# Two-layer hybrid decoder trunk on one core: standing halves of the last down projection 128 bytes apart, three transfers held back, the convolution's middle sums in tiles of their own, query and key weights at four places

## The chip, the cores and the metric

The kernel runs on one core of one Trainium2 chip. The metric is the device time of one execution in microseconds (us). Three runs of the kernel before took 1107.52, 1106.53 and 1103.94 us; the median is 1106.53. One execution was profiled, and all rows below come from it. TensorE (PE) multiplies; VectorE (DVE) and ScalarE (ACT) work on tiles in SBUF and PSUM; GpSimd (POOL) and SyncE (SP) mostly issue DMA transfers, each on a queue of its own.

## The reference, cut to what matters

512 tokens of width 1024 go through two layers in float32. Layer 0 mixes tokens with 16 attention heads, layer 1 with a gated short convolution. Both end in the same kind of MLP, with `w_up` of 1024 x 5632 and `w_down` of 2816 x 1024.

```python
proj = rms_norm(h, norm_g) @ w_in            # layer 0: queries, keys, values, 8 gates
h = h + attention(proj) @ w_out              # layer 0
y = gate_b * causal_dwconv(gate_c * u, conv_w)   # layer 1: gate_b, gate_c, u = thirds of xn @ w_in
h = h + y @ w_out                            # layer 1
u = causal_dwconv(rms_norm(h, ffn_norm) @ w_up, ffn_conv)   # both layers
h = h + (silu(u[..., :2816]) * u[..., 2816:]) @ w_down      # both layers
```

## The kernel before

**Products.** Every float32 operand of a large product is split into a high and a low half that PE can take: ACT copies the high half (`whi`, L327 or L1045), DVE subtracts it from the operand and leaves the low half (`wlo`, L328 or L1047). PE then makes three products for each pair of blocks: high with high, high with low, low with high. Of the two operands of a matmul one stands in the array (128 x 128), the other moves through it (128 x 256 or 128 x 512). In a row of the profile such as `psb<-act,whi` the operand that moves is named first, the one that stands last.

**Sevens.** The up projections, the convolution's input projection and the down projections work on 2 x 2 blocks with seven products in place of eight. In the class `Sevens` (both up projections and, under the name "c", the convolution) a group g of 128 output columns is seven slots named p1, p7, p3, p6, p2, q5, q4, of 24 matmuls of 128 x 256 each. The weights of each slot are sums of the four blocks of w: the tiles X, Y, Z and W of a group are loaded from DRAM, and the sums are made partly by DVE, partly by transfers that POOL issues and that add to what the tile holds. In the convolution (five groups, 0 to 4) the middle sum Y + X is made by DVE in the tile Y itself (L1162), between the split of p7 and POOL's transfer that adds to X; the slot q5 needs that X. W and Z go through the three buffers of the pool `raw`.

**Standing and moving.** In `Sevens` and in layer 0's down projection the weights stand and the activations move. In layer 1's down projection, the last stage, it is the other way: the activations (`act`, split by `operand`) stand, the weights move. The tile `act` holds its high and low halves 2048 bytes apart in both layers. The weight tiles `whi` and `wlo` are tiles of `CHUNK` = 1056 floats, 4224 bytes, and where `load` puts one of the two `ASIDE` = 32 floats in, the offset between halves moves by 128 bytes.

**Down projection.** Seven phases (one per product) of six steps (`GROUPS`, one or two blocks of 128 rows each, 11 blocks together), 132 matmuls of 128 x 256 a phase, 924 in all. In layer 0 the weights of the phase q4 for the steps 3 to 5 are brought by POOL as added transfers, while SP loads those of the phase p3.

**Order.** Each engine works in program order. A scheduler decides the order ahead of time from the instructions' place in the code, with `pin` and `behind` fixing some of it; `behind(a, b)` puts a after b.

**Stages of the profiled execution** (us from the span's start): attention to 255, its output projection and the norm to 275, layer 0's first up groups (plain) to 316, layer 0 up in `Sevens` to 490, layer 0 down to 603, convolution to 735, its output projection to 770, layer 1 up to 985, layer 1 down to 1103.

Of the kernel before, what the change touches and what calls it, by code (L numbers as in the profile page):

```python
# [57 lines left out]
def trunk(  # L58
# [208 lines left out]
    wanted, ready, at, halve, aside = [], [], [0], {}, set()  # L267
# [9 lines left out]

    def bring(i):
        place, nk, n, blocks, queue = wanted[i]
        raw = place()  # L280
        if raw is None:
            raw = wp.tile([P, CHUNK], F32, tag="raw", name=f"raw{i}")
        v = raw[:, 0:nk * n].rearrange("p (k c) -> p k c", c=n)
        for (dram, k0, c0), fresh in blocks:
# [5 lines left out]
            elif not fresh or queue:  # L290
                tc.keep_in_program_order(
                    nc.gpsimd.dma_start(v, src, **({} if fresh else {"accum_op": ALU.add})))
            else:
                nc.sync.dma_start(v, src)
# [8 lines left out]
    def load(i):  # L303

        hi, lo = weight_tiles(i)
        begins = (0, 0)
# [160 lines left out]
    def want_qk(p):  # L467
        want(w_in, 0, 8, D + p * P, P)
        want(w_in, 0, 8, p * P, P)
# [631 lines left out]
    class Sevens:  # L1101

        def __init__(self, name, mp, groups, block_of):
            self.name, self.mp, self.groups, self.block_of = name, mp, groups, block_of
            self.forms = {n: [mp.tile([P, 4, HT], F32R, tag=f"{n}_{i}", name=f"{n}_{i}{name}") for i in ("hi", "lo")] for n in FORMS}
            self.st, self.wides, self.table, self.scaled = {}, {}, None, False

# [50 lines left out]

        def first_sums(self, g):
            self.weights_of(g, "p7", "Y")  # L1160
            if not self.table:
                self.summed = dve.tensor_tensor(self.st[g]["Y"], self.st[g]["Y"], self.st[g]["X"], op=ALU.add)  # L1162
# [13 lines left out]
        def slot(self, g, s):  # L1176
# [21 lines left out]
            elif s == 1:  # L1198
                first = not was
                if on and first and not self.ahead and "p6" not in c:  # L1200
                    self.weights_of(g, "p6", "three" if self.table else "Y")
# [4 lines left out]
                if on and not first and not self.table:  # L1206
                    self.weights_of(g, "p6", "Y")
                if soon and not self.table:
                    self.add_block(g + 1, "Y", 1, 1)
            elif s == 2:  # L1210
                if on:
# [3 lines left out]
                    c["four"] = c["three" if self.table else "Y"]  # L1215
# [4 lines left out]
            elif s == 3:  # L1220
                if was:
                    self.early(p, st[p]["R"])
                if on:
                    self.weights_of(g, "q5", "X")
                    if not self.table:
                        self.kept(g, "Xs", c["R"])
                        self.weights_of(g, "q4", "four")
            elif s == 4:
# [5 lines left out]
            if s == 5:  # L1234
                if on:
                    self.load_one(g, "Z", self.block_of(g, 1, 1))
                    self.open_wides(g)
                    if soon and not self.table:
                        self.weights_of(g + 1, "p1", "X")
                    self.left(g, c["A"])  # L1240
# [10 lines left out]
        chores, credit, ahead = (), 0.0, False  # L1251
# [141 lines left out]
    def conv_seven(norm, mp, rp):  # L1393
# [6 lines left out]
        up.norm, up.chores, up.ahead = norm, [], True  # L1400
# [50 lines left out]
        def tail(p, s):  # L1451
            u, c = (wides[p][n] for n in ("yg", "yv"))
            if p == 4:
# [6 lines left out]
                elif s == 3:  # L1460
                    halves_in(6, 2)
# [7 lines left out]
            elif s in (3, 4):  # L1469
                if s == 3:  # L1470
                    dve.tensor_tensor(u, u, both(row2), op=ALU.mult)
                if p < 3 or s == 3:
                    conv(2 * p + s - 3, u[:, s - 3, :])
# [71 lines left out]
    def mlp(layer, norm, mp, begun_up=None):  # L1545
# [36 lines left out]
        if layer == 0:  # L1582
            want_conv()
# [5 lines left out]
        def operand(i):  # L1589
# [5 lines left out]
            t = acts[i] = mp.tile([P, 2, 2, HT], F32R, tag=act_tags[i % 4], name=f"act{layer}_{i}")  # L1595
# [238 lines left out]
```

## Time and profile before

| | |
|---|---|
| runs | 1107.52, 1106.53, 1103.94 us; median 1106.53 |
| profiled execution | 1107.02 us, of which the span is 1105.2 |
| PE busy | 1088.8 us, 99% of the span |
| DVE busy | 959.6 us, 87% |
| ACT busy | 685.3 us, 62% |
| POOL busy | 181.1 us, 16% |

The span is the time from the first to the last instruction that the profiler saw; 1.8 us lie outside it. PE has work nearly all the time, so a share of 99% does not tell whether it works at its best pace. Matmuls overlap: a row gives some 280 ns for one of 128 x 256, but they start about 113 ns apart. So the number of matmuls in a stretch tells more of PE than its busy time does.

### The profile page before, as it was taken

Reading aid. Unit: us, or ns where it says so; the run is one execution under the profiler, and the core shown is the slowest. Engines: PE = TensorE matmul, PEld = TensorE weight load, DVE = VectorE, ACT = ScalarE, POOL = GpSimd, SP = SyncE. Lnnn points to the kernel's source line nnn. Section 1 sums busy time; section 2 is a strip of 40 time slices with the busy share of each in tenths; the row PEclk is TensorE's granted clock in tenths of the full one; section 3 lists DMA queues with packets and bytes.
Section 4 is the critical chain, followed back from the end, with each engine's and each line's share of the span. In section 5 each row is a group of like instructions: output and inputs, shape, how many; then the busy total and the mean of one; then the engine's idle time right before and its main releaser. Section 6 shows DMA issues by size and latency. Waiting matters only on the chain.

```text
span 1105.2 us, 21688 instructions
## 1 busy us (share of the span) xinstructions
PE 1088.8 (99%) x8781; PEld 1034.4 (94%) x8781; DVE 959.6 (87%) x1482; ACT 685.3 (62%) x1020; POOL 181.1 (16%) x206
## 2 busy tenths in 40 slices
PE   9999999999999999999999999999999999999998
PEld 7888787879999999999999899999999999999998
DVE  5798898997898888899979889877899899999886
ACT  7466667655466776776547655445666656567653
POOL 4011111111012211014401001001121121114300
PEclk9999999999999999999999999999999999999999
DMA  7678867789667988899964865698879887799951
GB/s 198 168 186 194 206 169 186 197 213 238 190 149 196 215 193 217 210 259 225 236 177 110 202 166 127 132 277 190 209 195 215 184 209 184 214 276 206 233 143 58
DMA packets 178116, 214.21 MB, mean 194 GB/s; under 512 B 7676, under 2 KB 143916, under 8 KB 178016
## 3 DMA queue, kind: packets, MB, share of 16 engines
q0 software_dynamic: 53280, 95.34, 44.9%
q1 hardware_dynamic: 124576, 117.42, 33.4%
q8 instruction: 69, 1.13, 0.4%
q14 instruction: 31, 0.25, 0.1%
q10 hardware_dynamic: 160, 0.07, 0.0%
HBM read 205.72 MB, written 44.04 MB: 226 GB/s over the span
## 4 chain that ended last, share of the span: by engine, by line
PE 64%; DVE 15%; issue 12%; DMA 6%; ACT 2%; POOL 0%; DVEq 0%; POOLq 0%; ACTq 0%
PE psb L351 14%; PE psb L1096 12%; PE psb L1710 10%; PE psa L1710 8%; PE psa L1096 5%; PE psa L351 3%; DMA three<-in_ffn_w_up 3%; DVE wlo_p L1047 3%; PE psb L727 2%; DMA Xc<-in_conv_w_in 2%; PE psa L824 2%; DVE wlo L328 2%; PE psc L799 1%; DVE ug L460 1%; PE psb L609 1%
## 5 line engine op out<-in xcount | busy, mean ns | idle before, releaser
L1096 PE MATMUL psb<-p_hi,wlo_p 128*128 128x256 f32 x480 | 132.5, 276 | 0.9 <-DVE wlo_p L74 0.9
L1096 PE MATMUL psb<-p_lo,whi_p 128*128 128x256 f32 x480 | 132.6, 276 | 0.0
L1096 PE MATMUL psb<-p_hi,whi_p 128*128 128x256 f32 x480 | 132.6, 276 | 0.0
L327 ACT ACTIVATE whi<-raw 128x1024 fp32r<-128x1024 f32 (+2 forms) x77 | 78.9, 1026 | 67.1 <-PE psb L351 22.5
L328 DVE TENSOR_TENSOR wlo<-raw,whi 128x1024 fp32r<-128x1024 f32 (+2 forms) x77 | 90.9, 1180 | 23.4 <-ACT whi L327 20.1
L351 PE MATMUL psb<-hs_a,whi 128*128 128x512 f32 (+1 forms) x312 | 93.3, 369 | 0.0
L1096 PE MATMUL psa<-p_hi,wlo_p 128*128 128x256 f32 x320 | 90.0, 281 | 1.8 <-DVE wlo_p L1047 1.7
L1096 PEld LDWEIGHTS psb<-p_hi,wlo_p 128*128 128x128 f32 x480 | 90.0, 188 | 1.2 <-DVE wlo_p L74 1.2
L1096 PE MATMUL psb<-q_hi,wlo_q 128*128 128x256 f32 x320 | 89.3, 279 | 1.3 <-DVE wlo_q L1047 1.3
L1096 PEld LDWEIGHTS psb<-p_hi,whi_p 128*128 128x128 f32 x480 | 90.1, 188 | 0.0
L1096 PEld LDWEIGHTS psb<-p_lo,whi_p 128*128 128x128 f32 x480 | 90.1, 188 | 0.0
L1096 PE MATMUL psa<-p_hi,whi_p 128*128 128x256 f32 x320 | 89.2, 279 | 0.2 <-ACT whi_p L1045 0.2
L1096 PE MATMUL psb<-q_hi,whi_q 128*128 128x256 f32 x320 | 88.9, 278 | 0.2 <-ACT Xs L1157 0.2
L1096 PE MATMUL psa<-p_lo,whi_p 128*128 128x256 f32 x320 | 89.0, 278 | 0.0
L1096 PE MATMUL psb<-q_lo,whi_q 128*128 128x256 f32 x320 | 88.6, 277 | 0.0
L351 PE MATMUL psb<-hs_a,wlo 128*128 128x512 f32 (+1 forms) x208 | 69.5, 359 | 0.0
L1096 PEld LDWEIGHTS psa<-p_hi,wlo_p 128*128 128x128 f32 x320 | 60.6, 189 | 2.9 <-DVE wlo_p L1047 2.4
L351 PEld LDWEIGHTS psb<-hs_a,whi 128*128 128x128 f32 x312 | 52.4, 188 | 10.3 <-issue 3.2
L1096 PEld LDWEIGHTS psb<-q_hi,wlo_q 128*128 128x128 f32 x320 | 60.2, 188 | 1.9 <-DVE wlo_q L1047 1.7
L1710 PE MATMUL psb<-act,whi 128*128 128x256 f32 x352 | 60.9, 277 | 0.9 <-DVE act L1049 0.7
L1096 PEld LDWEIGHTS psa<-p_hi,whi_p 128*128 128x128 f32 x320 | 60.6, 190 | 0.4 <-ACT whi_p L1045 0.4
L1096 PEld LDWEIGHTS psb<-q_hi,whi_q 128*128 128x128 f32 x320 | 60.3, 189 | 0.6 <-ACT Xs L1157 0.4
(544 smaller groups left out, 3699.8 us busy)
## 6 DMA issues: line engine op xcount, KB each, us to landing
t<-in_ffn_w_up POOLq DMA_DIRECT2D x24, 768.0 KB, 7.8
raw<-in_attn_w_in SPq DMA_DIRECT2D x24, 512.0 KB, 4.8
t<-in_ffn_w_up POOLq DMA_DIRECT2D x12, 1024.0 KB, 10.2
X<-in_ffn_w_up SPq DMA_DIRECT2D x20, 512.0 KB, 5.0
Y<-t SPq DMA_DIRECT2D x20, 512.0 KB, 6.6
three<-t SPq DMA_DIRECT2D x20, 512.0 KB, 5.6
W<-in_ffn_w_up SPq DMA_DIRECT2D x20, 512.0 KB, 4.0
Z<-in_ffn_w_up SPq DMA_DIRECT2D x20, 512.0 KB, 5.5
```

Source lines behind the costliest of these rows:

```text
L327: return (act.activation(hi_, raw[:, at_], AF.Copy), dve.tensor_tensor(lo_, raw[:, at_], f32(hi_), op=ALU.subtract))
L328: dve.tensor_tensor(lo_, raw[:, at_], f32(hi_), op=ALU.subtract))
L351: made = [pe.matmul(acc[:, c], w[x], rhs[y][:, c], start=first and x + y + c.start == 0, stop=last and x == 1 and c.stop == S) for x, y in ...
L460: made.append(dve.scalar_tensor_tensor(dst[:, d:], src[:, 0:S - d], tap(j), dst[:, d:], op0=ALU.mult, op1=ALU.add))
L609: pe.matmul(acc, lhs[0], w[0], start=first, stop=False)
L727: pe.matmul(ss[e][:, c:c + wide], ql[rows, b * P:n], kl[rows, 0:wide], start=first and b == bs[0], stop=last and b == bs[-1])
L799: pe.transpose(t[:, k * P:(k + 1) * P], w[:, e, k * P:(k + 1) * P], ident)
L824: pe.matmul(out_, w, t[:, first:first + step * (NB - k - 1) + 1:step, :], start=k == 0 and i == 0, stop=k == NB - 1 and i == 1)
L1047: rest = dve.tensor_tensor(lo, src, f32(hi), op=ALU.subtract)
L1096: pe.matmul(to, w[a][:, k, c], x[b][:, k, :], start=fresh and i + k + t == 0, stop=i == 1 and k == 3 and t == 2, skip_group_check=not fresh)
L1710: pe.matmul(part, l, r[:, c], start=begin and o + t + c.start == 0, stop=end and t == 2 and o + c.start > 0, skip_group_check=not fresh)
```

## The change

1. In layer 1's down projection the two halves of the standing tile `act` are put 128 bytes further apart (2048 + 128), the high half first in every second step and the low half first in the others. In layer 1's up projection the forms p6 and p2 of the activations get the 128 bytes too (`form_tile`).
2. In layer 0's down projection POOL runs a tiny addition (`hold`) that reads the tile into which SP loads step 3 of the phase p3, ahead of the three transfers of q4. They are thus issued only when that load has landed.
3. In the convolution's groups 1, 2 and 3 the sum Y + X goes into a tile `three` from the pool `raw`, behind the split of p1 (`three_of`), so that POOL's added transfer to X no longer comes after a sum in Y, and `raw` holds three tiles a group where it held two. SP's loads change their order: X1, Y1, Z0, X2, Y2, W1, Y3 where it was X1, Y1, Z0, W1, Z1, X2, Y2. The convolution's tail waits behind the split of q4.
4. The last piece of the convolution's output is split by two instructions of 128 x 512 on each of ACT and DVE in place of one of 128 x 1024 (`halves_in(6, 1)`, `halves_in(7, 1)`).
5. The weight tiles of queries and keys start 0, 32, 64 or 96 bytes into their buffers, high and low half alike.
6. In the first `Sevens` group of layer 0 the weights of p2 are split in slot 1, not in slot 2.
7. In the first group of layer 1 the next group's p7 weights are split ahead of the join of yv (`begins`).

```diff
-                tc.keep_in_program_order(
-                    nc.gpsimd.dma_start(v, src, **({} if fresh else {"accum_op": ALU.add})))
+                added = nc.gpsimd.dma_start(v, src, **({} if fresh else {"accum_op": ALU.add}))
+                tc.keep_in_program_order(added)
+                if i in landed:
+                    hold, other = tiny.tile([P, 1], F32, tag="hold", name=f"hold{i}", bufs=1), raws[landed[i]][:, 0:1]
+                    held_ = pool.tensor_tensor(hold, other, other, op=ALU.add)
+                    behind(added, held_)
...
-        begins = (0, 0)
+        begins = (shifted.get(i, 0),) * 2
...
-        want(w_in, 0, 8, p * P, P)
+        for i in (1, 0):
+            shifted[len(wanted)] = 8 * ((p + 2 * i) % 4)
+            want(w_in, 0, 8, i * D + p * P, P)
...
-            self.forms = {n: [mp.tile([P, 4, HT], F32R, tag=f"{n}_{i}", name=f"{n}_{i}{name}") for i in ("hi", "lo")] for n in FORMS}
+            self.forms = {n: [self.form_tile(mp, n, i) for i in ("hi", "lo")] for n in FORMS}
             self.st, self.wides, self.table, self.scaled = {}, {}, None, False
+
+        def form_tile(self, mp, n, i):
+            if self.name == 1 and n in ("p6", "p2"):
+                t, c = mp.tile([P, CHUNK], F32R, tag=f"{n}_{i}", name=f"{n}_{i}{self.name}"), ASIDE if i == "lo" else 0
+                return t[:, c:c + 1024].rearrange("p (k c) -> p k c", c=HT)
+            return mp.tile([P, 4, HT], F32R, tag=f"{n}_{i}", name=f"{n}_{i}{self.name}")
...
+        def sum_of(self, g):
+            return "three" if self.table or g in self.aside else "Y"
+
+        def three_of(self, g):
+            c = self.st[g]
+            c["three"] = wp.tile([P, CHUNK], F32, tag="raw", name=f"three{self.name}{g}")[:, 0:1024].rearrange("p (k c) -> p k c", c=2 * P)
+            behind(dve.tensor_tensor(c["three"], c["Y"], c["X"], op=ALU.add), self.rest)
+
         def first_sums(self, g):
+            c = self.st[g]
             self.weights_of(g, "p7", "Y")
-            if not self.table:
-                self.summed = dve.tensor_tensor(self.st[g]["Y"], self.st[g]["Y"], self.st[g]["X"], op=ALU.add)
+            if not self.table and g not in self.aside:
+                self.summed = dve.tensor_tensor(c["Y"], c["Y"], c["X"], op=ALU.add)
             self.add_block(g, "X", 0, 1)
             if self.table:
                 self.load_one(g, "three", self.table("6", g))
...
+                if on and first and self.name == 0:
+                    self.weights_of(g, "p2", "W")
...
+                        if g + 1 in self.aside:
+                            self.three_of(g + 1)
...
+                begins = self.name == 1 and not was
+                if soon and begins:
+                    self.first_sums(g + 1)
                 if on:
                     self.join(g, "yv", c["R"], c["P7s"])
-                if soon:
+                if soon and not begins:
...
-        up.norm, up.chores, up.ahead = norm, [], True
+        up.norm, up.chores, up.ahead, up.aside = norm, [], True, (1, 2, 3)
...
-                    halves_in(6, 2)
+                    halves_in(6, 1)
+                    halves_in(7, 1)
...
+            landed[begun + 6 * len(GROUPS) + 3] = begun + 4 * len(GROUPS) + 3
...
-            t = acts[i] = mp.tile([P, 2, 2, HT], F32R, tag=act_tags[i % 4], name=f"act{layer}_{i}")
-            halves_to(t[:, 0, 0:nk, :], t[:, 1, 0:nk, :], blocks.block(name, k0, nk), sign, held=("act", "dve") if p else ())
+            t = mp.tile([P, CHUNK if layer else 1024], F32R, tag=act_tags[i % 4], name=f"act{layer}_{i}")
+            hi, lo = acts[i] = [
+                t[:, c:c + 2 * HT].rearrange("p (k c) -> p k c", c=HT)
+                for c in (((0, 2 * HT + ASIDE), (2 * HT + ASIDE, 0))[i % 2] if layer else (0, 2 * HT))]
+            halves_to(hi[:, 0:nk, :], lo[:, 0:nk, :], blocks.block(name, k0, nk), sign, held=("act", "dve") if p else ())
```

In DVE's program at layer 0's first `Sevens` group `hs_a_wide` are the causal convolution's partial results of plain columns, `W` the loaded weight block, `wlo_p` the low half that the slot p2 needs and `wlo_q` that of the slots q5 and q4. Before:

```order
L1362 TENSOR_TENSOR hs_a_wide_4104<-psc_3897,nrow_n_3618 128x512
L1362 TENSOR_TENSOR hs_a_wide_4104<-psc_3956,nrow_n_3618 128x512
L460 SCALAR_TENSOR_TENSOR hs_a_wide_4104<-hs_a_wide_4104,taps 128x511 x2
L460 SCALAR_TENSOR_TENSOR hs_a_wide_4104<-hs_a_wide_4104,taps 128x510 x2
L460 SCALAR_TENSOR_TENSOR hs_a_wide_4104<-hs_a_wide_4104,taps 128x511
L1047 TENSOR_TENSOR wlo_p_4096<-W_4053,whi_p_4095 128x1024
L1047 TENSOR_TENSOR wlo_q_4131<-X_3893,whi_q_4130 128x1024
L1083 TENSOR_TENSOR head_blocks_3462<-hs_a_wide_4104 128x256
```

After:

```order
L1392 TENSOR_TENSOR hs_a_wide_4104<-psc_3897,nrow_n_3618 128x512
L1392 TENSOR_TENSOR hs_a_wide_4104<-psc_3956,nrow_n_3618 128x512
L466 SCALAR_TENSOR_TENSOR hs_a_wide_4104<-hs_a_wide_4104,taps 128x511
L1054 TENSOR_TENSOR wlo_p_4094<-W_4053,whi_p_4093 128x1024
L466 SCALAR_TENSOR_TENSOR hs_a_wide_4104<-hs_a_wide_4104,taps 128x510
L466 SCALAR_TENSOR_TENSOR hs_a_wide_4104<-hs_a_wide_4104,taps 128x511 x2
L1054 TENSOR_TENSOR wlo_q_4131<-X_3893,whi_q_4130 128x1024
L466 SCALAR_TENSOR_TENSOR hs_a_wide_4104<-hs_a_wide_4104,taps 128x510 x2
```

The split of W has moved ahead of four of the five `SCALAR_TENSOR_TENSOR` operations, and the split of X of two.

In POOL's program in layer 0's down projection the tiles `q_hi_chain` and `q_lo_chain` receive the transfers for the phase q4, and `raw` is the tile that SP fills for step 3 of p3. Before, from the second transfer ahead of the three on:

```order
L292 DMA p_lo_chain_0_6381<-in_ffn_w_down 128x2x512
L292 DMA q_hi_chain_0_6423<-in_ffn_w_down 128x2x512
L292 DMA q_lo_chain_0_6457<-in_ffn_w_down 128x512
L292 DMA q_hi_chain_0_6492<-in_ffn_w_down 128x2x512
L292 DMA q_lo_chain_0_6527<-in_ffn_w_down 128x2x512
```

After:

```order
L293 DMA p_lo_chain_0_6381<-in_ffn_w_down 128x2x512
L293 DMA q_hi_chain_0_6423<-in_ffn_w_down 128x2x512
L297 TENSOR_TENSOR hold_7413<-raw_7037 128x1
L293 DMA q_lo_chain_0_6457<-in_ffn_w_down 128x512
L293 DMA q_hi_chain_0_6492<-in_ffn_w_down 128x2x512
L293 DMA q_lo_chain_0_6527<-in_ffn_w_down 128x2x512
```

The three transfers are the same ones; ahead of them stands one addition on a column of `raw`.

In DVE's program at the convolution's group 3, from its split of p1 on, `Xc`, `Yc` and `Zc` are its weight tiles and `hs_a_conv` and `y` belong to the group before. Before:

```order
L1047 TENSOR_TENSOR wlo_p1c_8433<-Xc_8270,whi_p1c_8432 128x1024
L1429 TENSOR_TENSOR hs_a_conv<-hs_a_conv,early 128x1024
L1150 TENSOR_TENSOR hs_a_conv<-psb_8299,P7sc_8331 128x2x256
L1047 TENSOR_TENSOR y_8429<-hs_a_conv,y_8429 128x1024
L1047 TENSOR_TENSOR wlo_p7c_8465<-Yc_8271,whi_p7c_8464 128x1024
L1150 TENSOR_TENSOR hs_a_conv<-psb_8274,Xsc_8367 128x2x256
L1162 TENSOR_TENSOR Yc_8271<-Yc_8271,Xc_8270 128x1024
L1047 TENSOR_TENSOR wlo_p3c_8496<-Zc_8430,whi_p3c_8495 128x1024
```

After:

```order
L1054 TENSOR_TENSOR wlo_p1c_8437<-Xc_8274,whi_p1c_8436 128x1024
L1459 TENSOR_TENSOR hs_a_conv<-hs_a_conv,early 128x1024
L1178 TENSOR_TENSOR threec_8440<-Yc_8275,Xc_8274 128x1024
L1163 TENSOR_TENSOR hs_a_conv<-psb_8303,P7sc_8335 128x2x256
L1054 TENSOR_TENSOR y_8433<-hs_a_conv,y_8433 128x1024
L1054 TENSOR_TENSOR wlo_p7c_8471<-Yc_8275,whi_p7c_8470 128x1024
L1054 TENSOR_TENSOR wlo_p3c_8501<-Zc_8434,whi_p3c_8500 128x1024
```

The addition of X and Y has moved from seventh to third place, into a tile of its own.

## Rows read from the trace of the kernel before

**Rows 1.** Page, busy time of the engines.

```profile
PE 1088.8 (99%) x8781; PEld 1034.4 (94%) x8781; DVE 959.6 (87%) x1482; ACT 685.3 (62%) x1020; POOL 181.1 (16%) x206
```

**Rows 2.** Chain that ended last: start, us, what; two down projections, queries and keys.

```profile
43.51 7.63 PE psb L351 x33
...
539.53 14.96 PE psb L1710 x132
...
1038.66 15.55 PE psb L1710 x132
```

**Rows 3.** Windows: length, then busy us (count) of PE, PEld, DVE, ACT, POOL; PEclk, DMA.

```profile
325.00:350.00 25.00, 23.04 (x186) 22.64 (x185) 20.95 (x28) 17.14 (x24) 3.73 (x3) 0.93 0.82 177
330.00:335.00 5.00, 5.00 (x32) 5.00 (x31) 4.60 (x7) 1.80 (x3) 0.00 (x0) 0.66 0.66 180
400.00:425.00 25.00, 25.00 (x223) 25.00 (x222) 20.17 (x26) 17.94 (x24) 4.75 (x4) 1.00 0.89 204
550.00:575.00 25.00, 23.60 (x205) 23.20 (x204) 20.68 (x28) 13.32 (x20) 1.20 (x1) 1.00 0.71 185
675.00:700.00 25.00, 24.64 (x209) 24.09 (x209) 22.27 (x25) 14.68 (x19) 2.59 (x2) 1.00 0.65 156
986.70:1011.70 25.00, 25.00 (x213) 25.00 (x213) 24.54 (x34) 17.70 (x26) 9.09 (x8) 1.00 1.07 242
1050.00:1075.00 25.00, 25.00 (x214) 25.00 (x213) 22.01 (x31) 13.07 (x19) 1.01 (x1) 1.00 0.61 158
```

**Rows 4.** PE's waits from 250 us on: us in total, times, longest.

```profile
PE psb L1096 <- DVE wlo_q L1047: 1.3, 2, 0.8
...
PE psb L1096 <- DVE wlo_p L74: 0.9, 1, 0.9
...
PE psa L351 <- DVE y_lo L1047: 0.5, 1, 0.5
```

**Rows 5.** Timeline of DVE and PE, layer 0's first Sevens group: start, us, what, [idle before].

```profile
325.06 3.39 DVE L460 SCALAR_TENSOR_TENSOR hs_a_wide<-hs_a_wide,taps 128x511 f32<-128x511 f32 x5
328.37 1.22 DVE L1047 TENSOR_TENSOR wlo_p<-W,whi_p 128x1024 fp32r<-128x1024 f32 x1
...
329.64 0.39 PE L1096 MATMUL psa<-p_hi,wlo_p 128*128 128x256 f32 x1 [1.72 <-DVE wlo_p L1047]
```

**Rows 6.** Timeline of POOL, SP and ACT, layer 0's down projection.

```profile
550.23 1.20 POOL L292 DMA_DIRECT2D q_lo_chain<-in_ffn_w_down  x1 [1.33 <-DVE wlo L328]
...
552.30 5.38 SPq L294 DMA_DIRECT2D raw<-in_ffn_w_down  x3
...
562.81 1.06 ACT L327 ACTIVATE whi<-raw 128x1024 fp32r<-128x1024 f32 x1 [3.37 <-DMA raw<-in_ffn_w_down]
...
590.15 0.62 ACT L327 ACTIVATE whi<-q_lo_chain 128x512 fp32r<-128x512 f32 x1
```

**Rows 7.** Timeline of DVE, POOL and ACT, convolution, group 3.

```profile
680.28 1.21 DVE L1429 TENSOR_TENSOR hs_a_conv<-hs_a_conv,early 128x1024 f32<-128x1024 f32 x1
...
685.50 1.22 DVE L1162 TENSOR_TENSOR Yc<-Yc,Xc 128x1024 f32<-128x1024 f32 x1
...
687.25 1.28 POOL L1123 DMA_DIRECT2D Xc<-in_conv_w_in  x1 [18.51 <-issue]
...
694.70 1.06 ACT L1045 ACTIVATE whi_q5c<-Xc 128x1024 fp32r<-128x1024 f32 x1 [5.29 <-DMA Xc<-in_conv_w_in]
```

**Rows 8.** Timeline of DVE, layer 1's first group.

```profile
789.95 0.69 DVE L74 TENSOR_TENSOR y_both<-psb,P7s 128x512 f32<-128x512 f32 x1
...
791.75 1.22 DVE L74 TENSOR_TENSOR wlo_p<-Y,whi_p 128x1024 fp32r<-128x1024 f32 x1
```

**Rows 9.** Timeline of SP and ACT, convolution; page, one kind of load.

```profile
675.47 0.37 SPq L1111 DMA_DIRECT2D Xc<-in_conv_w_in  x1
...
688.35 1.05 ACT L1045 ACTIVATE whi_p2c<-Wc 128x1024 fp32r<-128x1024 f32 x1
...
W<-in_ffn_w_up SPq DMA_DIRECT2D x20, 512.0 KB, 4.0
```

More of the change, by code (lines that the diff above doesn't have):

```diff
@@ L266, in trunk @@
     LEFT, RIGHT = slice(0, S // 2), slice(S // 2, S)
-    wanted, ready, at, halve, aside = [], [], [0], {}, set()
+    wanted, ready, at, halve, aside, shifted = [], [], [0], {}, set(), {}
     def want(dram, k0, nk, c0, n, *more):
@@ L276, in trunk @@
     brought = {}
+    raws, landed = {}, {}
     def bring(i):
@@ L281, in bring @@
         if raw is None:
-            raw = wp.tile([P, CHUNK], F32, tag="raw", name=f"raw{i}")
+            raw = raws[i] = wp.tile([P, CHUNK], F32, tag="raw", name=f"raw{i}")
         v = raw[:, 0:nk * n].rearrange("p (k c) -> p k c", c=n)
@@ L467, in want_qk @@
     def want_qk(p):
-        want(w_in, 0, 8, D + p * P, P)
-        want(w_in, 0, 8, p * P, P)
+        for i in (1, 0):
+            shifted[len(wanted)] = 8 * ((p + 2 * i) % 4)
+            want(w_in, 0, 8, i * D + p * P, P)
     def want_v(g):
@@ L1200, in slot @@
                 if on and first and not self.ahead and "p6" not in c:
-                    self.weights_of(g, "p6", "three" if self.table else "Y")
+                    self.weights_of(g, "p6", self.sum_of(g))
                 if on and not first and self.table:
@@ L1206, in slot @@
                 if on and not first and not self.table:
-                    self.weights_of(g, "p6", "Y")
+                    self.weights_of(g, "p6", self.sum_of(g))
+                if on and first and self.name == 0:
+                    self.weights_of(g, "p2", "W")
                 if soon and not self.table:
@@ L1214, in slot @@
                         self.weights_of(g, "p2", "W")
-                    c["four"] = c["three" if self.table else "Y"]
+                    c["four"] = c[self.sum_of(g)]
                     if self.table and soon:
@@ L1227, in slot @@
                         self.weights_of(g, "q4", "four")
+                        self.fourth = self.rest
             elif s == 4:
@@ L1245, in slot @@
             elif s == 6:
+                begins = self.name == 1 and not was
+                if soon and begins:
+                    self.first_sums(g + 1)
                 if on:
                     self.join(g, "yv", c["R"], c["P7s"])
-                if soon:
+                if soon and not begins:
                     self.first_sums(g + 1)
-        chores, credit, ahead = (), 0.0, False
+        chores, credit, ahead, aside = (), 0.0, False, ()
         def rate(self, g, s):
@@ L1472, in tail @@
                 if p < 3 or s == 3:
-                    conv(2 * p + s - 3, u[:, s - 3, :])
+                    made = conv(2 * p + s - 3, u[:, s - 3, :])
+                    behind(made[0], up.fourth)
             elif s == 5 and p < 2:
@@ L1704, in step @@
                             if layer:
-                                to, l, r = acc[b], acts[i][:, x, k, b * P:(b + 1) * P], w[y][:, k, :]
+                                to, l, r = acc[b], acts[i][x][:, k, b * P:(b + 1) * P], w[y][:, k, :]
                             else:
-                                to, l, r = acc[b][:, o * HT:(o + 1) * HT], w[y][:, k, (2 * b + o) * P:(2 * b + o + 1) * P], acts[i][:, x, k, :]
+                                to, l, r = acc[b][:, o * HT:(o + 1) * HT], w[y][:, k, (2 * b + o) * P:(2 * b + o + 1) * P], acts[i][x][:, k, :]
                             for c in (LEFT, RIGHT) if layer else (LEFT,):
```

## Prediction, made before the run

> **What bounds the kernel now.** I read the busy times first: PE works 99% of the span [rows 1]. That says only that PE is the engine to watch; where it loses time is read from how many matmuls start in a stretch. The windows give the measure: an undisturbed 25 us in layer 0's up projection hold 223 matmuls [rows 3]. Every matmul missing from that in a stretch of 128 x 256 matmuls is 25/223 = 0.112 us. By this count PE lost 37 x 0.112 = 4.1 us in 325 to 350 (186), 18 x 0.112 = 2.0 us in 550 to 575 (205), 1.6 us in 675 to 700 (209), and 1.0 us in 1050 to 1075 (214), though in the last one PE waited for nothing: busy 25.00 of 25.00 [rows 3]. So two kinds of loss are there, short waits in front of a slot whose weights are late, and a pace that is lower without any wait.
>
> The second kind is seen in the chain that ended last, which joins a phase's 132 matmuls of one shape. In layer 0's down projection they take 14.96 us, 113.3 ns each; in layer 1's 15.55 us, 117.8 ns each [rows 2]. PE's list of waits [rows 4] and the timelines around them [rows 5 to 8] give the first kind.
>
> I make the sum against the profiled execution, 1107.0 us, which is 0.5 us above the median of the three runs. The runs spread over 3.6 us, so about 0.3% (3.3 us) is what a measurement of this kernel can tell from no change.
>
> **Part 6, layer 0's first group.** DVE works off five STT operations in 3.39 us and only then, at 328.37, splits W; PE stands 1.72 us until 329.64 for it [rows 5]. The granted clock then fell: 0.66 of full speed over 330 to 335, between PE's two levels of 1.2 and 2.4 GHz, and 32 matmuls began there [rows 3]. Wait and clock make the 4.1 us. In the new order the split of W stands behind one STT: 325.06 + 0.68 = 325.7, done by 326.9, while PE began to wait at 329.64 - 1.72 = 327.9. The STTs that it passes come later: three of them stand between it and the split of X, which so starts at 326.9 + 3 x 0.68 = 328.9 in place of 329.50, and the next slot loses nothing. A wait not had brings no clock loss. I leave 0.3 us of it as lost: **-3.8 us**, bounds -4.1 and, if the wait only moves to the next slot, -2.
>
> **Part 2, the three transfers.** ACT stands 3.37 us until a raw tile of p3, that of step 4, has landed at 562.81 [rows 6], and PE loses its 2.0 us in that window [rows 3]. SP issued that and two more loads from 552.30 on, while POOL's added transfers, the last issued at 550.23, were still under way; ACT takes q4's tile only at 590.15 [rows 6]. Held back until step 3 of p3 has landed, 256 + 512 + 512 KB are out of the way of step 3, partly of steps 4 and 5. Step 3 lands before step 4's 562.8, so at least 590.15 - 562.8 = 27 us are left for the three, of the 40 that the last had; only beyond that would PE pay. Behind the hold stand these three on POOL, and then nothing that it does before the convolution. The hold itself is one addition on 128 x 1, POOL's shortest. I take **-1.6 us** (bounds -2.0, all of it, and 0, if steps 4 and 5 are as late as before).
>
> **Parts 3 and 4, the convolution.** In group 3 the sum stands at 685.50, POOL's addition to X starts at 687.25, and ACT waits 5.29 us for it at 694.70 [rows 7]. The new place is behind the split of p1 and one multiplication (680.28 + 1.21 = 681.5): 4.0 us earlier, so POOL's transfer too, and of ACT's wait 1.3 us are left. Group 3's window lost 1.6 us [rows 3]; I take 1.2 of it. Groups 1 and 2 wait in the same way for less, and I take a quarter of group 3's for each, 0.6 together. Group 4 isn't changed. The last split by halves lets PE start when the first half is there: the wait for `y_lo` was 0.5 us [rows 4], I take 0.4 at the cost of one more instruction on each of ACT and DVE, which have nothing else due there. **-2.2 us**, bounds -3.7 (1.6 for group 3, as much for groups 1 and 2 together, 0.5 for `y_lo`) and 0.
>
> **Part 7 and the new order of layer 1.** The split of Y stood behind the join and two multiplications, 789.95 to 791.75 [rows 8], and PE waited 0.9 us for it [rows 4]; ahead of the join it comes 1.8 us earlier: -0.8. Two groups waited for `wlo_q` 1.3 us together [rows 4]; the order puts the split that frees their tile `three` one STT (0.68 us, a fifth of 3.39 [rows 5]) earlier, so that 0.6 of the longest wait of 0.8 goes, and nearly all of the other: -0.9. Together **-1.7 us**, bounds -2.2 and 0.
>
> **Part 1, the pace of the last stage.** 4.5 ns x 924 matmuls = 4.1 us is the most there is [rows 2]. What differs between the two down projections: the fast one has weights standing, halves 4224 bytes apart, and the very `act` tiles with halves 2048 bytes apart moving; the slow one has those `act` tiles standing. So 2048 bytes between halves do no harm where these move; where they stand, they may, and the change takes just this away. It isn't the only difference: in the last stage two matmuls in a row use the same standing block. DVE is busy 24.54 of 25 us in 986.7 to 1011.7 [rows 3], so in the stage's first quarter a faster PE would partly wait for splits. I take three quarters, **-3.0 us**, bounds 0 and -4.1.
>
> The tiles of p6 and p2 in layer 1's up projection move, and moving halves 2048 bytes apart were fast above: no gain, and if the 128 bytes did harm there, 2 slots x 24 x 11 groups x 4.5 ns = 2.4 us. Taken as 0.
>
> **Part 5, queries and keys.** One of these 512-wide matmuls took 7.63/33 = 231 ns [rows 2], twice 115.6, between the two levels (226.7 and 235.6). 384 of them could win 1.7 us or lose 1.7 us. High and low half stay together, so nothing in the rows favours a side: 0.
>
> Sum: -3.8 - 1.6 - 2.2 - 1.7 - 3.0 = -12.3, and 1107.0 - 12.3 = **1094.7 us**.
>
> **Rivals.**
> The forecast case, waits mostly gone and pace up: 0.50.
>
> The pace doesn't depend on these addresses: the part's term is 0 and the time 1097.7. For it: one stage alone shows the slow level, and it differs in more than the distance. Against it: PE waits for nothing in 1050 to 1075 and DVE, at 22.01 of 25 us, isn't short there [rows 3]. Chance 0.22. The Trainium skill, page "TensorE: Matmul & The Clock Gate", section "Step-by-step: what each phase is for", says that PE reads the moving operand and the one to be loaded through two independent ports, so that loading doesn't take read bandwidth from the running matmul. By that rule where the standing halves lie would change nothing, and this rival holds; the trace shows a second level that the rule doesn't foresee, and no row yet shows its cause.
>
> The waits come back later: DVE, busy 20.95 of 25 us at 325 and 22.27 at 675 [rows 3], or the held transfers among the loads of the next phase, give back half of the 9.3 us: 1099.4. Chance 0.14; with the pace unchanged as well 1102.4, chance 0.08.
>
> Slower than before: `raw` now gives each of W, Z and `three` one buffer, and SP's load of W stands behind X. In group 3 that X was issued at 675.47 and W is taken at 688.35 [rows 9], 12.9 us later; such a load takes some 4 us [rows 9]. From 12.9 us on PE would lose what W is late. To outweigh 12.3 us and be seen (3.3 more), three groups must lose 5.2 us each, so W must take 18.1 us. The time would then be 1110.3. Chance 0.03.
>
> All terms at their far bounds and queries and keys faster (1107.0 - 17.8 = 1089.2): 0.03.
>
> **How the numbers follow.** From the cases: faster is all below 1103.2, that is all but the slow case and the 0.06 of the pair of failures that overshoot 1102.4: 0.91; within 0.3% 0.06; slower 0.03. The range leaves out, above, the two failures together and the slow case, and below the far bounds; with the tails of the cases inside, 8 in 10 are left: 1090.5 to 1100.5.
>
> **What would show it.** In the profile after: no PE wait for `wlo_p` in layer 0's first group and clock 1.00 there; some 220 matmuls in that window. ACT's wait for `raw` in layer 0's down projection under 1.5 us, q4's transfers issued between 553 and 563 and no wait of `whi` for a `q_lo_chain`. POOL's addition to X some 4 us earlier against the slot, and no wait for `wlo_q5c`. Last stage: phases of 132 matmuls in 15.0 us, not 15.5. The prediction is wrong if these phases stay at 15.5 and a new wait of several us appears in one of the stages, most likely at W in the convolution or at the loads behind the held transfers.

## The result, and the profile after

The changed kernel is **slower** by 0.4%: 1110.80 us (median of 20 runs, 1107.29 to 1113.32) against 1106.32 us of the kernel before on the same chip (20 runs, 1103.04 to 1108.88), ratio 1.0039 [1.0029, 1.0050]. The forecast was 1094.7 us, range 1090.5 to 1100.5. The execution of the changed kernel whose profile is shown is the shortest of its 20 (1107.29 us, span 1105.1), so a usual one should hold more waits than it shows; a second profile of the same code (e0) took 1112.88.

Windows of the changed kernel, columns as in [rows 3]:

```profile
325.00:350.00 25.00, 25.00 (x218) 24.66 (x217) 23.04 (x31) 18.42 (x27) 3.77 (x3) 1.00 0.88 200
550.00:575.00 25.00, 25.00 (x223) 25.00 (x222) 21.22 (x30) 14.01 (x20) 3.87 (x4) 1.00 0.73 187
675.00:700.00 25.00, 24.05 (x209) 23.63 (x208) 24.97 (x28) 15.04 (x18) 2.59 (x2) 1.00 0.54 126
800.00:825.00 25.00, 22.91 (x193) 22.11 (x192) 22.00 (x27) 15.28 (x19) 3.81 (x3) 1.00 0.71 167
825.00:850.00 25.00, 23.98 (x201) 23.19 (x200) 22.41 (x29) 13.38 (x17) 5.60 (x5) 1.00 0.83 211
1050.00:1075.00 25.00, 25.00 (x222) 25.00 (x221) 22.56 (x32) 13.91 (x20) 1.19 (x1) 1.00 0.67 174
```

And two of the kernel before:

```profile
800.00:825.00 25.00, 25.00 (x223) 25.00 (x223) 23.69 (x30) 16.22 (x21) 3.77 (x3) 1.00 0.79 190
825.00:850.00 25.00, 25.00 (x219) 24.85 (x218) 23.57 (x31) 14.33 (x17) 6.26 (x5) 1.00 0.85 208
```

In this profile the forecast stands at 325 (218 matmuls for 186), 550 (223 for 205) and 1050 (222 for 214); in e0's the window at 550 holds only 193. The loss stands where the prediction didn't look: 800 to 850, 193 and 201 matmuls where the kernel before had 223 and 219. PE's list of waits from 250 us on says for what:

```profile
PE psb L1103 <- DVE wlo_p L1054: 2.9, 6, 0.8
PE psb L1103 <- DVE wlo_q L1054: 2.4, 4, 0.8
PE psb L1103 <- ACT whi_q L1052: 1.9, 2, 1.7
```

The waits named in [rows 4] for `wlo_p` (0.9) and `y_lo` are gone, but six for `wlo_p` and one of 1.7 us for `whi_q` are new, all of them in layer 1's up projection. How far the kernel is ahead is read from a POOL transfer that both kernels issue, `X` in layer 1's first group and four groups later. Before, POOL's timeline:

```profile
787.01 1.29 POOL L1123 DMA_DIRECT2D X<-in_ffn_w_up  x1 [12.53 <-DVE wlo_p L74]
...
868.60 1.30 POOL L1123 DMA_DIRECT2D X<-in_ffn_w_up  x1 [0.22 <-issue]
```

After, with the transfers into `three` between them:

```profile
781.46 1.29 POOL L1136 DMA_DIRECT2D X<-in_ffn_w_up  x1 [12.54 <-DVE wlo_p L74]
792.73 1.28 POOL L1136 DMA_DIRECT2D three<-in_ffn_w_up  x1 [9.98 <-DVE wlo_p L1054]
...
814.94 1.28 POOL L1136 DMA_DIRECT2D three<-in_ffn_w_up  x1 [6.07 <-DVE wlo_p L1054]
...
835.83 1.28 POOL L1136 DMA_DIRECT2D three<-in_ffn_w_up  x1 [6.34 <-DVE wlo_p L1054]
...
856.93 1.29 POOL L1136 DMA_DIRECT2D three<-in_ffn_w_up  x1 [6.21 <-DVE wlo_p L1054]
...
868.50 1.30 POOL L1136 DMA_DIRECT2D X<-in_ffn_w_up  x1 [0.22 <-issue]
```

It enters layer 1 5.6 us ahead and four groups later is ahead by 0.1: the whole gain is lost there. At the last stage's phase of [rows 2] it is 1.2 us behind, and the last stage's faster pace gives that back. In the chain that ended last:

```profile
1039.86 15.04 PE psb L1746 x132
```

### The profile page after: what moved, and what is told of

Read it like the earlier page. It is cut to its first block, busy times and chain, and to the rows that moved or that the text cites. A ratio compares the mean times of both kernels' runs of the same rounds, so it can differ in the third digit from the quotient of the medians.

```text
span 1105.1 us, 21693 instructions
## 1 busy us (share of the span) xinstructions
PE 1086.6 (98%) x8781; PEld 1030.2 (93%) x8781; DVE 959.8 (87%) x1483; ACT 684.3 (62%) x1021; POOL 181.2 (16%) x207
## 4 chain that ended last, share of the span: by engine, by line
PE 70%; DVE 15%; issue 9%; DMA 4%; ACT 2%; POOL 0%; DVEq 0%; ACTq 0%; POOLq 0%
PE psb L1103 17%; PE psb L357 15%; PE psa L1746 8%; PE psb L1746 8%; PE psa L1103 6%; PE psa L357 4%; DMA three<-in_ffn_w_up 4%; DVE wlo_p L1054 3%; PE psb L734 2%; DVE wlo L334 2%; PE psa L831 2%; PE psc L357 1%; PE psc L806 1%; ACT whi L333 1%; DVE uv L466 1%
## 5 line engine op out<-in xcount | busy, mean ns | idle before, releaser
L334 DVE TENSOR_TENSOR wlo<-raw,whi 128x1024 fp32r<-128x1024 f32 (+2 forms) x77 | 90.8, 1179 | 20.7 <-ACT whi L333 20.5
```

Of the source, the lines that this page charges most:

```text
L334: dve.tensor_tensor(lo_, raw[:, at_], f32(hi_), op=ALU.subtract))
```

## The experiments

Each time is a median, with its ratio to runs of the kernel before on the same chip (medians 1108.06, 1106.31 and 1107.26 us for e0 to e3, e4 to e7, e8 to e11) and that ratio's 95% interval. 0.001 is 1.1 us. "Doubt" is the 95% half-width of a difference of two such ratios.

**e0, the changed kernel again**, no edit.

> The changed kernel once more, since its first profile fell on the shortest of its 20 runs (1107.3 against a median of 1110.8). All theories: 1108 to 1113 us. The theory that the order of layer 1's up projection is at fault expects PE to start layer 1's up projection some 5.5 us earlier than the kernel before did and to lose 8 us or more between 790 and 960 us, with the same waits for wlo_p and wlo_q as in the first profile; what differs from profile to profile should be the landing of single transfers into the tile three.

1112.44 us, 1.0043 [1.0026, 1.0059]: slower again.

**e1, the change without part 7.**

```diff
-                begins = self.name == 1 and not was
+                begins = False
```

> The changed kernel with part 7 taken out (the split of the next group's p7 weights stands behind the join of yv again, as before). On DVE and ACT this gives layer 1's up projection the order of the kernel before, row for row. Theory A (part 7 changes the order of the whole up projection and that costs the time): waits there fall back to some 3 us, the gains before it (5.6 us) and after it (2.6 us) stay, time 1097 to 1101. Rival B (the up projection is bound by the loop through the transfer into three, whatever the order, and swallows an earlier start): 1104 to 1108. Rival C (the tiles of p6 and p2, 128 bytes apart now, slow the matmuls): the waits stay as they are in the changed kernel, 1107 to 1111.

1105.96 us, 0.9974 [0.9956, 0.9992]. Part 7 costs 1112.44 - 1105.96 = 6.5 us (7.6 by the ratios). The rest gains only 2.1 us (2.9 by the ratio), so something else in it loses as well.

**e2, part 7 alone**, in the kernel before.

```diff
+                begins = self.name == 1 and not was
+                if soon and begins:
+                    self.first_sums(g + 1)
...
-                if soon:
+                if soon and not begins:
```

> The kernel before with part 7 alone. Theory A: slower by 5 to 9 us, 1111 to 1115, with waits for wlo_p in each of the first groups of layer 1's up projection. Rivals B and C: within 2 us of the kernel before (1.1 us at most gained by the first group's wait, which goes).

1114.74 us, 1.0064 [1.0042, 1.0086]: +7.1 by the ratio, the same loss from the other side.

**e3, part 1 alone**: `form_tile` and the larger `act` tiles of the diff above, in the kernel before.

```diff
...
+            hi, lo = acts[i] = [
+                t[:, c:c + 2 * HT].rearrange("p (k c) -> p k c", c=HT)
+                for c in (((0, 2 * HT + ASIDE), (2 * HT + ASIDE, 0))[i % 2] if layer else (0, 2 * HT))]
...
```

> The kernel before with part 1 alone (standing halves of the last stage 128 bytes further apart, tiles of p6 and p2 too); no engine's order changes. Theory A: the phases of the last stage take 15.0 us in place of 15.55, 2.5 to 4 us faster, 1102.5 to 1104. Rival C: layer 1's up projection loses 2.4 us or more and the kernel is the same or slower, 1106 to 1109.

1105.65 us, 0.9982 [0.9968, 0.9997]: -2.0 by the ratio.

**e4, part 2 alone**: the hold, in the kernel before.

```diff
+            landed[begun + 6 * len(GROUPS) + 3] = begun + 4 * len(GROUPS) + 3
```

> The kernel before with part 2 alone (the hold ahead of three of q4's transfers). As predicted at first: 1.6 us faster. Theory A (the hold opens as soon as step 3's load has landed, near 554, so all three transfers now run against step 5's load, issued near 557): step 3 and step 4 land some 5 us earlier, ACT then waits 3 us or more for step 5's tile at 560 to 566, PE loses 1 to 3 us there plus up to 1.7 us of half clock; 0 to 3 us slower. Rival B (the landing of step 5 only varies by chance): no change and no waits other than those of the kernel before.

1109.48 us (12 runs; the ratio leaves out one of 1333.77 us), 1.0025 [1.0007, 1.0042]: the hold loses 2.8 us by itself. Its timelines of POOL, SP and ACT, and the window, show why:

```profile
553.03 0.51 POOL L296 TENSOR_TENSOR hold<-raw 128x1 f32<-128x1 f32 x1 [10.69 <-DMA raw<-in_ffn_w_down]
...
550.23 5.38 SPq L299 DMA_DIRECT2D raw<-in_ffn_w_down  x3
...
564.16 1.06 ACT L332 ACTIVATE whi<-raw 128x1024 fp32r<-128x1024 f32 x1 [4.80 <-DMA raw<-in_ffn_w_down]
...
550.00:575.00 25.00, 22.91 (x184) 22.51 (x183) 18.63 (x26) 11.93 (x17) 3.84 (x4) 0.93 0.72 181
```

The hold opens at 553.0, when step 3 has landed, and the three transfers go out at 553.5 to 554.8, while SP's next loads are under way (three issues from 550.23 on). Step 3's and step 4's loads land 2.7 and 3.8 us after their issue (6.1 and 8.3 in the kernel before), but ACT's wait of 3.37 us for step 4 [rows 6] is now one of 4.80 us for step 5; the window holds 184 matmuls, 21 fewer than before [rows 3], at a granted clock of 0.93.

**e5, parts 3 and 4 alone**: the change with all other parts undone.

```diff
-            if self.name == 1 and n in ("p6", "p2"):
+            if False:
...
-                begins = self.name == 1 and not was
+                begins = False
...
-            landed[begun + 6 * len(GROUPS) + 3] = begun + 4 * len(GROUPS) + 3
```

(Taken out in the same way: `shifted`, the early split of W, and the larger `act` tiles.)

> The kernel before with parts 3 and 4 alone (middle sums in tiles of their own in the convolution's groups 1 to 3, the last split by halves). As predicted: 2.2 us gained between 640 and 740 us, and 2 us in the total. Theory A: the gain in the stage shows (2 to 4 us in the profile by the time layer 1's up projection begins), but half or more of it is lost in the up projection, whose groups wait for the transfer into three; total 0 to 2 us faster. Rival: slower, because W and Z come late.

1102.73 us, 0.9967 [0.9954, 0.9980]: -3.6, more than the -2.2 forecast.

**e6, without part 7, the hold on step 5's load.**

```diff
-            landed[begun + 6 * len(GROUPS) + 3] = begun + 4 * len(GROUPS) + 3
+            landed[begun + 6 * len(GROUPS) + 3] = begun + 4 * len(GROUPS) + 5
...
-                begins = self.name == 1 and not was
+                begins = False
```

> The changed kernel without part 7, and with the hold waiting for step 5's load of p3 in place of step 3's. Theory A: ACT's wait for step 5's tile goes, PE loses less than 1 us between 555 and 570, against 3 to 4 us in e1; total 1102 to 1105, some 2 us below e1. Rival B: as e1, within 1 us; or slower, because the three transfers then meet the loads that DVE adds (other) and these come late at 575 to 590.

1100.40 us, 0.9939 [0.9920, 0.9958], below every forecast. POOL and ACT:

```profile
560.91 0.73 POOL L297 TENSOR_TENSOR hold<-raw 128x1 f32<-128x1 f32 x1 [16.66 <-DMA raw<-in_ffn_w_down]
...
562.00 1.06 ACT L333 ACTIVATE whi<-raw 128x1024 fp32r<-128x1024 f32 x1 [1.14 <-PE psa L1746]
```

The tile that e4 waited for until 564.16 is taken at 562.00, and ACT waits for PE there, not for a load.

**e7, without part 7 and without the hold.**

```diff
-            landed[begun + 6 * len(GROUPS) + 3] = begun + 4 * len(GROUPS) + 3
...
-                begins = self.name == 1 and not was
+                begins = False
```

> The changed kernel without parts 7 and 2: parts 1, 3, 4, 5 and 6 are left. Theory A: PE's waits in layer 0's down projection are those of the kernel before (some 2 us at 563), total 1103 to 1106, 0 to 2 us below e1. Rival (the hold gains 1.6 us): 1.6 us above e1.

1100.58 us, 0.9937 [0.9915, 0.9959]. Against e1 the hold on step 3 costs 0.0037, 4.1 us (doubt 3.1). Against e6 the times show no gain of the hold on step 5 over none (0.0002, doubt 0.0029). e6 and e7 beat the kernel before by 6.7 and 7.0 us; no other kernel was faster.

**e8, e6 with part 7**, and in layer 1's first group `P7s` stays behind `ug` on ACT, as without part 7 (`last_act[0]` is the last activation of `causal_conv`).

```diff
...
-            act.activation(t, acc, AF.Copy)
+            made = act.activation(t, acc, AF.Copy)
+            if self.name == 1 and n == "P7s" and g - 1 in self.groups:
+                behind(made, last_act[0])
...
```

> The kernel of e6 (parts 1, 3 to 6, hold on step 5) with part 7 put back, and one order more: in layer 1's up projection ACT keeps P7s behind the activations that begin ug, so that in the first group these don't wait for P7s as in the changed kernel. The later groups keep the order that part 7 brings (splits of the next group's X between the last STTs, behind the split of three). Theory A1 (P7s ahead of ug on ACT in the first group makes the transfer into three late, and that lateness goes through the groups): as e6 or 1 us faster, 1099 to 1101. Theory A2 (the order of the later groups costs it, since the loop from one transfer into three to the next has become longer by two STTs): 4 to 6 us slower than e6, 1104 to 1107.

1107.17 us, 0.9997 [0.9985, 1.0008]: 0.0058 above e6, 6.4 us. What is lost doesn't lie in the place of `P7s` on ACT.

**e9, part 6 alone**, in the kernel before.

```diff
+                if on and first and self.name == 0:
+                    self.weights_of(g, "p2", "W")
```

> The kernel before with part 6 alone. As predicted: 3.8 us faster. Theory A (the stall at 327 goes, 3.7 us are won by 357, but by 390 one to three of them are lost in the next groups, which then wait for the transfer into three): 0.5 to 2.5 us faster. Rival: all of it is lost, same time.

1107.85 us, 1.0006 [0.9993, 1.0019]: no gain. Its windows, and POOL and ACT behind the place:

```profile
325.00:350.00 25.00, 24.86 (x217) 24.47 (x216) 23.25 (x31) 17.93 (x26) 3.89 (x4) 1.00 0.85 196
350.00:375.00 25.00, 24.23 (x211) 23.83 (x210) 19.45 (x26) 16.40 (x21) 5.65 (x5) 1.00 0.78 184
...
361.93 1.29 POOL L1123 DMA_DIRECT2D three<-in_ffn_w_up  x1 [3.97 <-DVE wlo_p L1047]
...
370.44 1.06 ACT L1045 ACTIVATE whi_q<-three 128x1024 fp32r<-128x1024 f32 x1 [3.21 <-DMA three<-in_ffn_w_up]
```

The same rows of the kernel before:

```profile
350.00:375.00 25.00, 25.00 (x223) 25.00 (x222) 21.27 (x28) 17.06 (x23) 5.04 (x4) 1.00 0.81 194
...
364.21 1.29 POOL L1123 DMA_DIRECT2D three<-in_ffn_w_up  x1 [4.54 <-DVE wlo_p L1047]
...
371.24 1.06 ACT L1045 ACTIVATE whi_q<-three 128x1024 fp32r<-128x1024 f32 x1 [1.17 <-DMA three<-in_ffn_w_up]
```

The window at 325 gains 31 matmuls [rows 3], the next loses 12. The transfer into `three` is issued 2.3 us earlier than before and taken only 0.8 earlier: it took 8.5 us from issue to ACT, where it took 7.0.

**e10, e6 without part 1**: `if False:` in `form_tile`, and the small tile back.

```diff
-            t = mp.tile([P, CHUNK if layer else 1024], F32R, tag=act_tags[i % 4], name=f"act{layer}_{i}")
+            t = mp.tile([P, 1024], F32R, tag=act_tags[i % 4], name=f"act{layer}_{i}")
...
```

> The kernel of e6 without part 1 (parts 3 to 6 and the hold on step 5). If part 1 gains what its phases show (13 to 15 ns per four matmuls, some 3 us in the last stage): 1103 to 1104. If part 1 also makes the transfer into three late in one group of layer 1's up projection, which took 8 to 9 us in five of six profiles with it and 6 in those without: that transfer takes 6 us here, and the kernel is within 1.5 us of e6, 1100 to 1102.

1103.37 us, 0.9965 [0.9950, 0.9981]: 0.0026 above e6, so part 1 is worth 2.9 us there (doubt 2.7).

**e11, part 1's larger tiles, halves 2048 bytes apart as before**: e3 with

```diff
-                for c in (((0, 2 * HT + ASIDE), (2 * HT + ASIDE, 0))[i % 2] if layer else (0, 2 * HT))]
+                for c in (0, 2 * HT)]
```

(and the same in `form_tile`).

> The kernel of e3 with its larger tiles (4224 bytes in place of 4096) but the halves where they were before, 2048 bytes apart. If the distance of the standing halves sets the pace: phases of 15.5 us again and the time of the kernel before. If it is only where the tiles lie, or something else of part 1: phases of 15.0 us. If the larger tiles are what makes the transfer into three late in one group, it takes 8 us or more here too, and the kernel is 1 to 3 us slower than before.

1105.82 us, 0.9989 [0.9974, 1.0004]: the time alone doesn't settle it. The pace does. Two rows of the chain that ended last of e10, then one of e11:

```profile
1000.05 12.24 PE psb L1744 x108
...
1033.21 15.55 PE psb L1744 x132
```

```profile
1036.48 15.08 PE psb L1719 x132
```

e11's phase, the fourth of the last stage, runs at the fast pace with the halves at the old distance. e10, with the small tiles, has both levels in one execution: 12.24 / 108 = 113.3 ns in the second phase, 117.8 ns in the fourth.

## Why the prediction was wrong, step by step

The terms measured alone add up to +0.6 (6) + 2.8 (2) - 3.6 (3 and 4) + 7.1 (7) - 2.0 (1) = +4.9 us, against the measured +4.3 (0.0039 x 1106). The five intervals together leave the sum open by some 4 us either way, so it doesn't show what each part does. The stages do. The table gives the time from PE's first matmul of a stage to that of the next, in the 14 profiles (range, median, number of profiles):

| stage | part | with it, us | without it, us |
|---|---|---|---|
| all ahead of layer 0's `Sevens` | 5 | 318.6 to 320.6, 319.0 (7) | 318.2 to 319.0, 318.7 (7) |
| layer 0 up, `Sevens` | 6 | 171.1 to 173.9, 172.3 (8) | 171.2 to 172.8, 172.8 (6) |
| layer 0 down | 2 | 133.3 to 138.1, 137.0 (4) | 134.0 to 136.8, 134.9 (7) |
| layer 0 down, hold on step 5 | | 133.1 to 133.3, 133.3 (3) | |
| convolution, its output projection | 3, 4 | 140.6 to 140.8, 140.7 (8) | 142.8 to 146.4, 144.5 (6) |
| layer 1 up | 7 | 221.2 to 225.2, 223.3 (4) | 214.6 to 219.7, 216.0 (10) |
| layer 1 down, to the end | 1 | 116.8 to 118.2, 117.3 (7) | 118.5 to 119.6, 118.9 (6) |

e11, with the larger tiles alone, has 116.9 in the last stage. The medians differ by +0.3, -0.5, +2.1, -3.8, +7.3 and -1.6 us, +3.8 together, so each part acts in its own stage much as it did alone, and the sign comes from parts 7 and 2. The ranges lie apart for parts 3 and 4, 7 and 1; for 2, 5 and 6 they overlap.

**Part 7 failed, -1.7 forecast, +6.5 measured (e0 less e1; e2 and e8 agree).** The 1.8 us at layer 1's first group were right: the split of Y stands at 784.33, and PE's wait of 0.9 us for it is gone. The error is the sentence "the order puts the split that frees their tile `three` one STT earlier". I read the new order at that one place. In the next three groups, though, the splits of `X` and of the q4 tile have STTs (DVE's `SCALAR_TENSOR_TENSOR` rows) between and behind them that stood ahead before. DVE in the changed kernel, one group and the start of the next:

```profile
800.77 1.23 DVE L1054 TENSOR_TENSOR wlo_q<-three,whi_q 128x1024 fp32r<-128x1024 f32 x1 [2.53 <-ACT whi_q L1052]
801.91 0.75 DVE L466 SCALAR_TENSOR_TENSOR uv<-y_both,taps,uv 128x511 f32<-128x511 f32 x1
802.57 1.22 DVE L1054 TENSOR_TENSOR wlo_p<-X,whi_p 128x1024 fp32r<-128x1024 f32 x1
803.71 0.74 DVE L466 SCALAR_TENSOR_TENSOR uv<-y_both,taps,uv 128x510 f32<-128x510 f32 x1
...
813.42 1.22 DVE L1054 TENSOR_TENSOR wlo_p<-three,whi_p 128x1024 fp32r<-128x1024 f32 x1
...
821.66 1.23 DVE L1054 TENSOR_TENSOR wlo_q<-three,whi_q 128x1024 fp32r<-128x1024 f32 x1 [1.24 <-ACT whi_q L1052]
...
834.32 1.22 DVE L1054 TENSOR_TENSOR wlo_p<-three,whi_p 128x1024 fp32r<-128x1024 f32 x1
```

ACT in the first of these groups, then ACT and DVE three groups later:

```profile
799.67 1.06 ACT L1052 ACTIVATE whi_q<-three 128x1024 fp32r<-128x1024 f32 x1 [2.53 <-DMA three<-in_ffn_w_up]
800.64 0.71 ACT L462 ACTIVATE uv<-y_both,taps 128x512 f32<-128x512 f32 x1
...
860.15 1.32 ACT L462 ACTIVATE uv<-y_both,taps 128x512 f32<-128x512 f32 x2
...
860.89 2.74 DVE L466 SCALAR_TENSOR_TENSOR uv<-y_both,taps,uv 128x511 f32<-128x511 f32 x4
```

The same stretch of e6, whose layer 1 has the order of before:

```profile
796.69 2.07 DVE L466 SCALAR_TENSOR_TENSOR uv<-y_both,taps,uv 128x511 f32<-128x511 f32 x3
798.68 1.22 DVE L1054 TENSOR_TENSOR wlo_q<-three,whi_q 128x1024 fp32r<-128x1024 f32 x1
...
810.54 1.22 DVE L1054 TENSOR_TENSOR wlo_p<-three,whi_p 128x1024 fp32r<-128x1024 f32 x1
...
818.94 1.23 DVE L1054 TENSOR_TENSOR wlo_q<-three,whi_q 128x1024 fp32r<-128x1024 f32 x1 [0.18 <-ACT whi_q L1052]
...
829.80 1.22 DVE L1054 TENSOR_TENSOR wlo_p<-three,whi_p 128x1024 fp32r<-128x1024 f32 x1
```

In e6 the STTs run in one piece while the transfer is under way; in the changed kernel DVE stands idle for that transfer (2.53 and 1.24 us) and does two of them afterwards. It couldn't do them earlier: they add to what ACT's second `uv` writes, and that stands behind ACT's split of `three`, which waits for the transfer. So ACT's order changed with DVE's.

These rows belong to a loop: POOL's transfer into `three`, ACT's and DVE's split of it for q4, their work up to the split of the next group's `three` for p6, and behind that POOL's next transfer. No buffer closes this loop (the next group's `three` is loaded from 794.26 on, ahead of the split at 800.77); the program order of ACT and DVE does. From the one split to the other it takes 12.65 us twice (800.77 to 813.42, 821.66 to 834.32), in e6 11.86 and 10.86. POOL's transfers into `three` come 22.2, 20.9 and 21.1 us apart in the changed kernel; in e6 they come

```profile
791.60 1.28 POOL L1136 DMA_DIRECT2D three<-in_ffn_w_up  x1 [7.94 <-DVE wlo_p L1054]
...
812.07 1.28 POOL L1136 DMA_DIRECT2D three<-in_ffn_w_up  x1 [6.84 <-DMA Z<-in_ffn_w_up]
...
831.32 1.28 POOL L1136 DMA_DIRECT2D three<-in_ffn_w_up  x1 [6.63 <-DVE wlo_p L1054]
...
850.81 1.29 POOL L1136 DMA_DIRECT2D three<-in_ffn_w_up  x1 [6.61 <-DVE wlo_p L1054]
```

20.5, 19.3 and 19.5 us apart. PE needs about 19 us for a group (seven slots of 24 matmuls at 113.3 ns each [rows 2]). So the loop was a second bound right behind PE, and the new order put it ahead. Another 2.1 us go in the first group, between the transfers at 767.61 and 792.73 (25.1 us, in e6 23.0), where the split for p6 stands behind one STT more.

Order and period go together within one execution. From the fourth group on both `uv` of ACT (860.15) and all four STTs of DVE (860.89) stand ahead of the split again, and the next transfer comes after 19.7 us. In e8 the old order is back one group sooner, and its periods are 21.8, 21.2 and 19.6 us. e8 also rules out the place of `P7s`. ACT's order wasn't tried apart from DVE's, nor which of the moved instructions costs most.

**Part 2 failed, -1.6 forecast, +2.8 alone and 4.1 within the change (e4; e1 against e7).** The wait at step 4 did go, as forecast. The step that failed is "out of the way of step 3, partly of steps 4 and 5": the hold opens on the first of three loads that SP has issued in a row, so the three transfers run beside the last of these, and step 5 loses more than step 4 gains. My bound of 0 took for granted that these steps could be no later than before. The idea that transfers of q4 must not run beside SP's loads is right in the stage: a hold on step 5 makes it shorter than in any profile without a hold. In the time of the whole kernel e6 and e7 show no difference.

**Part 6 failed, -3.8 forecast, nothing measured (e9).** In the changed kernel every row up to 350 us came as forecast: split of W at 325.75, of X at 328.87, clock 1.00. The step that failed is "I leave 0.3 us of it as lost": I followed the gain to the next slot only. Two groups later most of it is lost in the loop of `three`, here in layer 0. From issue to landing that transfer takes 8.3 to 10.5 us in the eight profiles with part 6 and 7.6 or less in the six without, and PE needs 20.3 to 23.8 us for the group in place of 19.0. What slows the transfer isn't shown. And of the 4.1 us not all is lost in every execution of the kernels without part 6. The same wait in e4, without part 6:

```profile
325.00:350.00 25.00, 23.05 (x200) 22.64 (x200) 22.33 (x30) 18.70 (x25) 3.13 (x3) 1.00 0.89 200
```

PE stands just as long there as before (busy 23.05 and 23.04 us [rows 3]), but the clock doesn't fall and 14 more matmuls fit in, 1.6 us. The rival that waits come back later was right in kind; I had given it half of the gain.

**Parts 3 and 4 were right in sign and too small, -2.2 forecast, -3.6 measured (e5).** POOL's addition to X in group 3 was forecast 4.0 us earlier against the slot. After, on DVE, POOL and ACT:

```profile
678.56 1.22 DVE L1178 TENSOR_TENSOR threec<-Yc,Xc 128x1024 f32<-128x1024 f32 x1
...
680.31 1.28 POOL L1136 DMA_DIRECT2D Xc<-in_conv_w_in  x1 [17.11 <-ACT y L1052]
...
687.89 1.06 ACT L1052 ACTIVATE whi_q5c<-Xc 128x1024 fp32r<-128x1024 f32 x1 [0.83 <-PE psb L1103]
```

ACT's 5.29 us for X [rows 7] are gone, and the slower case, W late, isn't there: `whi_p2c` isn't waited for. Group 3's window still holds 209 matmuls, with new waits of 0.5 and 0.4 us for `wlo_p7c` and `whi_p3c`. So the gain lies elsewhere than I had put most of it. By PE's time for a group, group 1 takes 19.0 us in all eight profiles with these parts and 19.6 to 23.3 in the six without; group 4, which I had left out, 18.9 against 19.3 to 20.6; group 3 only 20.6 against 20.3 to 21.7. I had sized the term from one execution, and it has the shortest convolution stage of those six (142.8 us).

**Part 1 was right in sign, -3.0 forecast, -2.0 (e3) and -2.9 (e10 against e6) measured, -1.6 in its stage, and its reason fell.** A phase takes 15.04 us, as forecast. But I named the distance between the halves, and e11 has the fast pace without it. (That the weight tiles' halves lie 4224 bytes apart, no row shows; it is the size of one tile.) What remains of part 1 in e11 is that the tiles are larger, so that those behind begin at other addresses, and the fourth phase is fast in all eight profiles with larger tiles and slow in the six without. But the places of the standing tiles can't be all: the same four tiles serve every phase, and e10 has both levels. What sets the level isn't shown. The rule of the Trainium skill weighed in the prediction (page "TensorE: Matmul & The Clock Gate", section "Step-by-step: what each phase is for", two independent read ports) names no second pace; 15.55 against 15.08 us shows one, and no run here shows whether the reads of the standing operand cause it.

**Part 5 as forecast, 0**: it wasn't run alone, but it is the only part that acts ahead of layer 0's `Sevens`, and the table shows no gain there. The 33 matmuls of [rows 2] take 7.68 us in the changed kernel, 7.63 before.

## What to carry to other kernels

Before a split or a load is moved, write down the loop of each tile that a transfer adds to (transfer, split, the engines' work up to the next group's split, next transfer) and its period beside PE's time for a group: a loop as long as PE's time makes earlier starts worthless and later ones expensive. Where a scheduler fills in the rest, compare the order of every engine over every repetition of the loop, since a change in one early group can rearrange several that follow. A hold must wait for the last transfer that it is to protect, not for the first, and be tried against no hold. What a wait costs is better read from several executions than from one.

## What the runs showed of the hardware

- PE's pace has two levels without any wait at granted clock 1.00, 113.3 to 114.2 ns (12.24 us for 108, 15.04 and 15.08 for 132) and 117.8 ns. Both occur in one execution with the same standing tiles (e10), and larger tiles with the same instructions bring a phase from the slower to the faster (e11). What sets the level is open.
- A stall doesn't always bring the clock down. The same 2.0 us missing from PE's busy time came with a granted clock of 0.93 over the window before [rows 3] and of 1.00, the level of 2.4 GHz, in e4. At 550 to 575, after waits of 1.1 and 1.0 us, e4 had 0.93, so it stood at the level of 1.2 GHz for a part of it; in e0, after waits of 1.6 and 1.0 us there, the window stayed at 1.00.
- The transfer into `three` near 915 us took from 5.9 to 9.2 us from POOL's issue to landing. It took 7.9 us or more in five of the seven profiles that have part 1's offset and not in e11 or the profiles without part 1. In those five PE needed 21.5 to 24.2 us for the group, in the other nine 19.3 to 20.0. Whether that is the placement or chance is open.
